# Another order of rows for the first part of x: which 24 KB row of DRAM goes to which partition

## The chip, the cores and the metric

The kernel runs on one core of one Trainium2 chip. The metric is device time in microseconds (us) of one execution; for the kernel before, three runs gave a median of 123.88 us (123.86 to 124.13). The profile is that of one further execution.

## The reference

```
x: (16, 512, 768) f32, A: (768, 16) f32, B: (16, 768) f32, scale = 0.5
out = x + scale * ((x @ A) @ B)        # f32
```

Flattened, x and out have 8192 rows of 768 numbers, 3 KB each. The kernel reads 25.2 MB and writes 25.2 MB.

## The kernel before

The 8192 rows are 64 tiles of 128 rows (one row per partition), and the tiles are taken in five parts of 8, 8, 16, 16 and 16 tiles (PARTS). A part of S tiles is laid out so that partition p holds S consecutive rows of DRAM: in the first two parts 8 rows, which are one run of 24 KB, in the others 16 rows, 48 KB. All of this is in one helper, memory(t2, i, s, n) (L92 to L94), which turns "part i, tiles s to s+n" into a pattern over DRAM; loads of x and stores of out both use it, so a row is stored where it was read.

x_sb has room for 48 tiles. The last part therefore goes into the room of the first two parts once these have been stored.

All transfers are issued by SP, in the order written by hand in on_sync, and one queue takes them in that order:

- the first part of x in two loads: tiles 0 and 1 (6 KB of each partition's 24 KB), then tiles 2 to 7 (18 KB of it); line L135
- A in three small loads of four 4 KB rows (L150) and B in one load of sixteen 3 KB rows (L154); both go to partitions 8 apart
- the second part of x in one load of 24 KB per partition, the third in two such loads, the fourth in one of 48 KB per partition (L135)
- the store of the first part and that of the second, each after the sum of its tiles is done (L143)
- the two loads of the fifth part, each after one of these stores has landed (L135)
- the stores of the third, fourth and fifth parts, 48 KB per partition (L143)

Every load has a semaphore of its own. The other engines work on groups of 8 tiles. For each group, POOL and ACT cast x to f16 (L179), half a group each; DVE transposes the copy in blocks of 32 (L237); TensorE projects it with A into y_ps (L268); ACT scales y and spreads it over a block diagonal y_bd (L225); TensorE multiplies by B into PSUM (L289); DVE adds the result to x in place (L242). A group's work needs no particular row in a particular partition: it treats the 128 rows of a tile alike.

Of the kernel before, what the change touches and what calls it, by code (L numbers as in the profile page):

```python
# [14 lines left out]


GROUP = 8

SUB = 4

# [4 lines left out]
def kernel(  # L25
# [10 lines left out]
    P = 128  # L36
# [7 lines left out]
    NC = D // 64  # L44
    NG = sum(PARTS) // GROUP
    PAIRS = GROUP // 2
    assert sum(PARTS) * P == T and NG * GROUP == sum(PARTS)
    sc = float(scale)


    def sb(name, shape, dtype):
        return nc.alloc_sbuf_tensor(name, shape, dtype).ap()

    def ps(name, shape):
        return nc.alloc_psum_tensor(name, shape, fp32).ap()
# [14 lines left out]
    b_mm = sb("b_mm", [P, D], MM_DT)  # L70
    xn = sb("xn", [P, GROUP, D], MM_DT)
    xt = sb("xt", [P, GROUP, D], MM_DT)
    y_bd = sb("y_bd", [P, GROUP, P], MM_DT)
    lora = [ps(f"lora_ps{i}", [P, 2, D]) for i in range(2)]
# [9 lines left out]
    parts = []  # L84
# [6 lines left out]

    def memory(t2, i, s, n):  # L92
        S = PARTS[i]
        return t2[ds(parts[i], S * P), :].rearrange("(p s) d -> p s d", s=S)[:, ds(s, n), :]  # L94

    def held(i, s, n):
        return tiles(where.index((i, s)), n)
# [34 lines left out]
    def on_sync(e):  # L132
        def load(k):
            ld = LOADS[k]
            e.dma_start(out=held(*ld), in_=memory(x2, *ld)).then_inc(s_load[k], 16)  # L135

        def store(k, done):
            st = STORES[k]
            e.wait_ge(s_sum, k + 1)
            if STORED[k] + 1 < NG:  # L140

                e.sem_inc(s_free[PAIRS - 1], 1)  # L142
            e.dma_start(out=memory(out2, *st), in_=held(*st)).then_inc(done, 16)  # L143
# [226 lines left out]
```

## Time and profile before

| what | value |
|---|---|
| median of three runs | 123.88 us |
| the profiled execution's own time | 123.84 us |
| its span, first to last instruction | 122.0 us |
| TensorE busy | 52.3 us (43%) |
| VectorE (DVE) busy | 81.7 us (67%) |
| ScalarE (ACT) busy | 37.5 us (31%) |
| GpSimd (POOL) busy | 28.8 us (24%) |
| moved by DMA | 50.43 MB in 1928 packets |

The span is 1.8 us shorter than the time, since the time also holds what lies ahead of the first and behind the last instruction. Each transfer of x or out consists of 128 packets, one per partition, of 6, 18, 24 or 48 KB; a core has 16 DMA engines, so an engine moves eight packets of each transfer. The trace records for each packet when it started, how long it took and its size, but not which engine or partition it belongs to. In the groups and in the chain, "SPq" is SP issuing a transfer, and "DMA" is the time from issue to landing, the wait in the queue included.

### The profile page before, as it was taken

The numbers are of one execution on the slowest core, as the hardware profiler recorded it, in microseconds if no ns is written. First come the engines' busy times: TensorE is split into PE (matmuls) and PEld (weight loads), VectorE is DVE, ScalarE is ACT, GpSimd is POOL, SyncE is SP. The second block draws the span as 40 slices with busy tenths as digits, with TensorE's granted clock in tenths as the row PEclk, the third lists the DMA queues.
The fourth block names the chain that finished last, engine by engine and source line by source line (L and its number), as shares of the span: only waits on it lengthen the run. The fifth ranks groups of instructions, "written<-read, shape, count | busy, mean of one in ns | idle before, by whom it ended". The sixth has DMA issues, their size and how long they took to land.

```text
span 122.0 us, 887 instructions
## 1 busy us (share of the span) xinstructions
PE 52.3 (43%) x322; PEld 30.4 (25%) x322; DVE 81.7 (67%) x42; ACT 37.5 (31%) x43; POOL 28.8 (24%) x26
## 2 busy tenths in 40 slices
PE   0000229487457647746745735974674340000000
PEld 0000016253233424424423322642442110000000
DVE  0002950599999999999999989999995991000000
ACT  4002938526409312734440093553004000000000
POOL 7731657127009002604400080530000000000000
PEclk9999999999999999999999996899999955555555
DMA  3999999999997996999999999998998998899890
GB/s 56 431 435 399 443 443 403 443 443 403 516 483 322 483 516 266 459 419 411 459 427 427 443 419 459 451 516 354 419 516 371 403 516 387 387 516 403 371 516 0
DMA packets 1928, 50.43 MB, mean 413 GB/s; under 512 B 236, under 2 KB 236, under 8 KB 392
## 3 DMA queue, kind: packets, MB, share of 16 engines
q1 hardware_dynamic: 1928, 50.43, 96.9%
HBM read 25.26 MB, written 25.17 MB: 413 GB/s over the span
## 4 chain that ended last, share of the span: by engine, by line
DMA 39%; DVE 28%; PE 7%; ACT 3%; issue 3%; POOL 2%; SPq 0%; DVEq 0%
DMA x_sb<-in_x_dram 20%; DMA out_dram<-x_sb 18%; DVE x_sb L242 18%; DVE xt L237 10%; PE ps_yt L268 5%; ACT xn L179 3%; POOL xn L179 2%; PE lora_ps L289 1%; SPq L135 0%; SPq L365 0%; DVEq L255 0%; SPq L130 0%; SPq L142 0%
## 5 line engine op out<-in xcount | busy, mean ns | idle before, releaser
L242 DVE TENSOR_TENSOR x_sb<-x_sb,lora_ps 128x1536 f32<-128x1536 f32 x32 | 53.7, 1735 | 1.4 <-PE lora_ps L289 1.4
L289 PE MATMUL lora_ps<-b_mm,y_bd 128*128 128x512 f16 (+1 forms) x128 | 26.6, 343 | 22.5 <-issue 14.8
L179 ACT CAST xn<-x_sb 128x3072 f16<-128x3072 f32 (+1 forms) x9 | 23.4, 2609 | 36.3 <-DMA x_sb<-in_x_dram 23.7
L268 PE MATMUL ps_yt<-xt,w_bd 128*128 128x256 f16 x192 | 26.5, 291 | 11.4 <-DVE xt L237 11.4
L237 DVE STREAM_TRANSPOSE xt<-xn 128x3072 f32<-128x3072 f32 (+1 forms) x9 | 27.1, 3006 | 6.3 <-PE ps_yt L268 5.5
L179 POOL CAST xn<-x_sb 128x3072 f16<-128x3072 f32 (+1 forms) x8 | 20.7, 2588 | 44.9 <-PE ps_yt L268 22.9
L268 PEld LDWEIGHTS ps_yt<-xt,w_bd 128*128 128x128 f16 x192 | 19.1, 102 | 19.4 <-issue 14.5
L289 PEld LDWEIGHTS lora_ps<-b_mm,y_bd 128*128 128x128 f16 x128 | 11.1, 100 | 35.8 <-issue 17.9
L225 ACT ACTIVATE y_bd<-ps_yt 32x256 f16<-32x256 f32 x32 | 12.0, 375 | 18.6 <-PE ps_yt L268 18.3
L230 DVE STREAM_TRANSPOSE a_t<-a_rows 96x1024 f32<-96x1024 f32 x1 | 1.9, 1946 | 11.5 <-DMA a_rows<-in_A_dram 11.5
L301 PE MATMUL lora_ps<-b_half,pick 128*128 128x512 f16 (+1 forms) x2 | 0.8, 500 | 12.8 <-POOL b_half L197 12.8
L301 PEld LDWEIGHTS lora_ps<-b_half,pick 128*128 128x128 f16 x2 | 0.1, 105 | 12.8 <-issue 12.8
L207 POOL COPY w_bd<-w_one 32x384 f16<-32x384 f16 x4 | 2.0, 502 | 0.2
L197 POOL CAST b_half<-b_rows 128x768 f16<-128x768 f32 x1 | 0.8, 829 | 4.7 <-DMA b_rows<-in_B_dram 4.7
L179 ACT ACT_TABLE_LOAD x1 | 1.3, 1283 | 0.9 <-SPq L130 0.9
L201 POOL CAST w_one<-a_t 32x128 f16<-32x128 f32 x3 | 1.2, 396 | 1.0 <-DVE a_t L230 0.9
L187 POOL MEMSET w_bd<- 128x1536 f32 x1 | 1.4, 1380 | 0.0
L184 POOL MEMSET a_rows<- 96x1024 f32 x1 | 0.9, 948 | 0.5 <-SPq L130 0.5
L218 ACT CAST b_mm<-lora_ps 128x768 f16<-128x768 f32 x1 | 0.8, 800 | 0.0
L185 POOL MEMSET b_rows<- 128x768 f32 x1 | 0.7, 735 | 0.0
L188 POOL MEMSET y_bd<- 128x512 f32 x1 | 0.5, 522 | 0.0
L190 POOL TENSOR_SCALAR_AFFINE_SELECT pick<-pick 128x128 f16<-128x128 f16 x1 | 0.3, 307 | 0.0
(5 smaller groups left out, 0.6 us busy)
## 6 DMA issues: line engine op xcount, KB each, us to landing
out_dram<-x_sb SPq DMA_DIRECT2D x3, 6144.0 KB, 23.6
x_sb<-in_x_dram SPq DMA_DIRECT2D x5, 3072.0 KB, 14.6
x_sb<-in_x_dram SPq DMA_DIRECT2D x1, 6144.0 KB, 41.9
out_dram<-x_sb SPq DMA_DIRECT2D x2, 3072.0 KB, 21.2
x_sb<-in_x_dram SPq DMA_DIRECT2D x1, 2304.0 KB, 10.0
x_sb<-in_x_dram SPq DMA_DIRECT2D x1, 768.0 KB, 4.6
a_rows<-in_A_dram SPq DMA_DIRECT2D x3, 16.0 KB
b_rows<-in_B_dram SPq DMA_DIRECT2D x1, 48.0 KB, 7.7
```

Source lines behind the costliest of these rows:

```text
L179: ins = copy(out=xn[:, ds(first, n), :], in_=tiles(t, n))
L184: e.memset(a_rows[0 : NC * APART], 0.0).then_inc(s_ready, 1)
L187: e.memset(w_bd.rearrange("p c k m -> p (c k m)").bitcast(fp32), 0.0)
L201: e.tensor_copy(out=w_one[:, ds(b * EACH, EACH), :, :], in_=a_t[ds(b * Q, Q)].rearrange("i k r (c n) -> i c k r n", n=APART)[..., 0],).the ...
L207: e.tensor_copy(out=w_bd[ds(b * Q, Q), :, :, ds(b * Q, R)], in_=w_one).then_inc(s_w, 1)
L225: last = e.mul(out=y_bd[q, :, q], in_=y_ps[q, :, :], mul=sc)
L230: e.transpose(out=a_t[0 : NC * APART].rearrange("i k r c -> i (k r) c"), in_=a_rows[0 : NC * APART].rearrange("c (i k r) -> c (k r) i", k= ...
L237: return e.transpose(out=ts[0], in_=ts[1])
L242: ins = e.tensor_tensor(out=xs, in0=xs, in1=lora[p % 2], op=mybir.AluOpType.add)
L268: mm = e.matmul(y_ps, w_bd[:, c, k, :], xv[:, :, c, :, k], start=(m == 0), stop=(m == MMS - 1),)
L289: mms.append(e.matmul(t[:, k, ds(n0, w)], y_bd[:, 2 * p + k, :], b_mm[:, ds(n0, w)], start=True, stop=True,))
L301: last = e.matmul(lora[0][:, 0, ds(n0, w)], pick.rearrange("p b r -> p (b r)"), b_half[:, ds(n0, w)], start=True, stop=True,)
```

## The change

In the helper, the first part (i == 0) gets another pattern. Its 128 runs of 24 KB are counted as j * 16 + e, with e from 0 to 15 and j from 0 to 7, and run j * 16 + e goes to partition e * 8 + j. So runs that are neighbours in memory go to partitions 8 apart, and one partition block of eight takes every sixteenth run. Both loads and the store of the first part change alike; nothing else does. The bytes of each packet, the number of transfers and their order on SP are as before; the pattern on the DRAM side has an outer dimension of 16 (24 KB apart) and a next one of 8 (384 KB apart) where it had one of 128.

```diff
 GROUP = 8
+
+
+ENG = 16
...
     def memory(t2, i, s, n):
         S = PARTS[i]
-        return t2[ds(parts[i], S * P), :].rearrange("(p s) d -> p s d", s=S)[:, ds(s, n), :]
+        rows = t2[ds(parts[i], S * P), :]
+        if i == 0:
+            return rows.rearrange("(j e s) d -> e j s d", s=S, e=ENG)[:, :, ds(s, n), :]
+        return rows.rearrange("(p s) d -> p s d", s=S)[:, ds(s, n), :]
```

## The prediction

> **What bounds the kernel now.** I read the page's DMA rows first, then the stretches of the span, then SP's issues and SP's waits.
>
> ```profile
> DMA  3999999999997996999999999998998998899890
> q1 hardware_dynamic: 1928, 50.43, 96.9%
> ```
>
> One queue keeps the sixteen DMA engines busy in 96.9% of the span. The row of tenths is low only in the first and the last slice. By stretch (the last two columns are the DMA share and GB/s; a share over 1 means that packets overlap):
>
> ```profile
> 0.00:2.00 2.00, 0.00 (x0) 0.00 (x0) 0.00 (x0) 1.09 (x1) 1.25 (x6) 1.00 0.04 6
> 2.00:4.70 2.70, 0.00 (x0) 0.00 (x0) 0.00 (x0) 0.19 (x1) 2.67 (x5) 1.00 1.04 335
> 4.70:10.00 5.30, 0.00 (x0) 0.00 (x0) 0.00 (x0) 0.00 (x0) 1.62 (x2) 1.00 0.98 419
> 10.00:47.00 37.00, 20.25 (x122) 12.02 (x123) 29.58 (x15) 17.68 (x18) 12.27 (x11) 1.00 1.01 429
> 47.00:54.50 7.50, 4.93 (x34) 2.80 (x32) 7.50 (x5) 4.25 (x5) 2.75 (x1) 1.00 1.03 442
> 54.50:120.60 66.10, 27.16 (x169) 15.59 (x168) 44.65 (x24) 14.26 (x19) 8.25 (x3) 0.80 0.99 425
> ```
>
> I cut at transfers: 2.0 to 4.7 is the first load, 4.7 to 10.0 the second, 47.0 to 54.5 the store of the first part, by the packet records. From 10 us on the rate hardly moves, for loads and stores alike. The packet records say why: 18 KB packets take 0.686 us (lowest and median alike), 24 KB packets 0.916, 48 KB packets 1.81, all about 27 GB/s per engine, with hardly any spread. Only the first load is slower: its first sixteen packets, one per engine, take 0.37 to 1.18 us, on average 0.77, where later ones take 0.234.
>
> So the end is set by the transfers from 2.0 us to 120.6 us, and a microsecond added to any of them is added to the end. What could hide it is a wait of the queue for its issuer:
>
> ```profile
> SPq L142 <- DVE x_sb L242: 55.0, 3, 26.1
> SPq L143 <- DVE x_sb L242: 17.6, 1, 17.6
> ```
>
> SP waits for DVE's sums, but is early even so: the chain of waits has the first store issued at 32.9, and its packets start at 47.0, 14.1 us later; the last store is issued at 101.0, and packets of the one before it run to 106.1. So the engines' work has 5 us or more to spare, and it moves along when the loads do. It hides nothing that is added to a transfer, and stays hidden itself.
>
> **The change, part by part.** It touches three transfers of 128 packets, eight per DMA engine: load one, 8 x 0.234 = 1.87 us at the settled rate; load two, 8 x 0.686 = 5.49; the first store, 8 x 0.916 = 7.33. Together 14.7 us of the 118.6 us of transfers. Packets, bytes, instructions of the other engines and SP's order are the same. TensorE, VectorE, ACT and POOL gain and lose nothing.
>
> *Issue.* The pattern of the first part no longer has 128 rows on both sides. The nearest rows are the issues of x (same form on both sides) and those of A and B, with short patterns:
>
> ```profile
> L135 SPq DMA_DIRECT2D x_sb<-in_x_dram x2: 383/398/412, 1.0 to 1.4; - x2
> L150 SPq DMA_DIRECT2D a_rows<-in_A_dram x3: 577/595/757, 1.9 to 3.4; - x3
> L154 SPq DMA_DIRECT2D b_rows<-in_B_dram x1: 542/542/542, 4.0 to 4.0; - x1
> ```
>
> If the new pattern is issued like those of A, an issue costs 595 - 398 = 0.2 us more (bounds: nothing, and 757 - 383 = 0.37). Only the first load's counts: nothing runs ahead of it. Load two's lies beside load one's data; the issues of A, B and the rest (4.0 to 6.6) lie beside load two's, which lasts to 10; the store's has its 14.1 us. Term: **+0.2**.
>
> *Rate of the three transfers.* What changes is who moves what. [...] With 16 outside on the DRAM side, I assume that an engine's share is one e: eight partitions in a row, 8e to 8e+7. The flat durations of before fit sixteen engines that each end in a place of their own. If partitions share entrances into SBUF, blocks of eight in a row may put two engines on one entrance at a time while others stand empty, since all sixteen walk through their blocks in step; each packet then takes twice its row. The trace can't show this directly: it has no engine or partition numbers, and no x transfer with this share.
>
> [...]
>
> Bounds from rows. Upper end: every packet doubles, +14.7. Lower end: nothing, by the row that speaks against: B's sixteen packets go to partitions 8 apart, one from each block of eight, and the records have 14 of them at 0.121 us and two at 0.21, so no doubling as a rule; but they are 3 KB each and spread over 0.9 us, too small and scattered to stand in each other's way for long. Below nothing: the first sixteen packets lose 0.77 - 0.234 = 0.53 us on average, which is all that a friendlier order in DRAM could win, since everything later runs at its settled rate.
>
> I take the upper end, since the loads are the opposite of B: 6 to 24 KB per packet, back to back, all engines in step. From it goes what engines out of step save. The first sixteen packets end between 2.36 and 3.28 us; two engines drawn from such a spread differ by a third of 0.92, 0.3 us. If a pair meets afresh in each half of each of three transfers, that is 6 x 0.3 = 1.8 us; but the end waits for the pair closest in step, so I take half, 0.9. Term: +14.7 - 0.9 = **+13.8**. The later transfers are not slowed: their share is the old one.
>
> Sum, against the profiled execution: 123.84 + 0.2 + 13.8 = **137.8 us**; the median of the runs shown is 0.04 above that execution, which changes nothing.
>
> **Rivals.**
>
> *Collisions on one side only.* Writing into SBUF is slowed, reading from it for the store is not, or the other way round. Loads alone: 123.84 + 0.2 + 7.4 - 0.6 = 130.8; the store alone: 123.84 + 0.2 + 7.3 - 0.3 = 131.0. For it: loads and stores have the same packet times, so the rows can't tell which side sets them. Against it: the same engines and partitions in both.
>
> *The rate stays.* Either the engines keep their old share (the change does not do what it says), or two engines in one block do not hinder each other. Then only the issue is left: 123.84 + 0.2 = 124.0, at most 124.6 if the first packets also start 0.4 us later. For it: B's packets. Against it: nothing in the trace is like the new share under full load.
>
> *Faster.* At the start sixteen engines read addresses 24 KB apart, one stretch of 384 KB, instead of places far apart. If that is what makes the first packets late, up to 0.53 us comes back: 123.84 + 0.2 - 0.53 = 123.5. It decides from the point where it wins more than the issue's 0.2 plus 0.25, so only if nearly all of the loss goes. For it: the slow first sixteen packets. Against it: they look like a first answer from memory, and any order has one.
>
> **How the numbers follow.** Two runs differ by 0.25 us (0.2%) without a cause, so within that counts as the same. Chances: collisions both ways 0.50 (134 to 141: the upper end is the full doubling, plus the 0.37 us issue, plus 2 us for engines that meet others still in the next transfer); one side only 0.16 (126 to 134); the rate stays 0.21, of which 0.11 within 0.25 us and 0.10 slower by more; faster 0.13. So slower 0.50 + 0.16 + 0.10 = 0.76, same 0.11, faster 0.13. The range runs from 123.9, which leaves out "faster" and about half of "same" (0.18), to 141 (0.02 above). The likeliest case's own range is 134 to 141.
>
> **What would show it.** Right: packets of 6, 18 and the store's 24 KB at about twice 0.234, 0.686 and 0.916 us; GB/s near 215 in the stretches of the three transfers, with the DMA share still near 1; the second load landing near 18 us instead of 11.4; later stretches at 425 to 429 GB/s. Issue: the first L141 issue (the load's line then) at 0.6 us instead of 0.4. Wrong: flat packets as before, or a slow start alone; then only the first slices differ, and the time is 123.3 to 124.6.

## The result, and the profile after

The changed kernel takes 137.75 us (median of six runs, 137.23 to 138.79) beside 123.93 for the kernel before on the same chip: 1.112 times as long, interval 1.109 to 1.115. The profiled execution is the longest of the six: 138.79 us, with a span of 137.0. Times and ratios in this document are of fast runs alone; only the kernel with the pattern in all five parts had others, two of six at 217.3 and 219.1 us.

Its page shows the same queue, the same packets and bytes, and DMA engines that are as busy as before. Only the rate has changed, in two places (40 slices of 3.4 us):

```profile
DMA  2998999999999998998999999999999999999970
GB/s 48 273 242 183 198 398 409 445 438 431 409 459 459 459 459 344 344 266 179 337 445 337 373 445 438 366 445 431 431 445 431 416 431 459 445 416 431 431 316 14
q1 hardware_dynamic: 1928, 50.43, 95.8%
```

Counted from 0, slices 1 to 4 hold the two loads of the first part, slices 15 to 18 its store. Busy is not fast here: the DMA row reads 9 in slice 4, at 198 GB/s, as it does in slice 7, at 445. Cut at these transfers, by stretch (the five busy times are those of PE, PEld, DVE, ACT and POOL, each with its count of instructions; then the granted TensorE clock, the DMA share and GB/s):

```profile
2.40:6.20 3.80, 0.00 (x0) 0.00 (x0) 0.00 (x0) 0.00 (x0) 2.42 (x5) 1.00 1.16 273
6.20:17.50 11.30, 0.00 (x0) 0.00 (x0) 0.00 (x0) 0.00 (x0) 1.46 (x1) 1.00 1.00 214
17.50:54.00 36.50, 19.97 (x127) 12.03 (x128) 30.37 (x16) 17.68 (x18) 12.26 (x11) 1.00 0.99 425
54.00:67.00 13.00, 8.18 (x56) 4.91 (x57) 13.00 (x7) 7.00 (x6) 5.50 (x2) 1.00 1.01 278
67.00:92.00 25.00, 10.88 (x58) 6.27 (x56) 16.56 (x9) 5.75 (x9) 2.75 (x1) 0.74 1.01 408
```

The second load (6.2 to 17.5) runs at 214 GB/s where it had 419; the loads behind it are back at 425; the store (54 to 67) runs at 278 where it had 442; and behind the store the rate stays a little low. In the packet records the 18 KB packets went from a median of 0.686 us to 1.43, the 6 KB ones from 0.234 to 0.40, the store's 24 KB ones from 0.912 to 1.47. Eight idle engines beside eight at the old packet times would give half the GB/s too, but the longer packets and the DMA share of 1.00 in the second load exclude that. The first two issues are longer too (383/398/412 ns before):

```profile
L141 SPq DMA_DIRECT2D x_sb<-in_x_dram x2: 573/625/677, 1.0 to 1.7; - x2
```

SP still waits for DVE's sums, and they are still early enough: the last store is issued at 115.6, and the sixteen engines land the one before between 118.2 and 121.6.

Most of the 15.0 us by which the profiled span grew can be added up from the packet records, eight packets per engine and transfer: first packet 0.45 later (1.99 to 2.44); load one 8 x (0.419 - 0.323) = 0.8; load two 8 x (1.387 - 0.692) = 5.6; the store 8 x (1.463 - 0.913) = 4.4; the transfers of 24 KB packets in the second part and the fifth part's loads, together 2.1 (means of 0.97 to 1.00 instead of 0.91 to 0.95); and in the last store the slowest engine lands 2.1 behind the mean of the sixteen instead of 0.7, 1.4 more. Sum 14.7, with unrounded terms; the remaining 0.3 is not accounted for.

### The profile page after: what moved, and what is told of

Same layout as the page of the kernel before. It is cut to its first block, busy times and chain, and to the rows that moved or that the text cites. A ratio compares the mean times of both kernels' runs of the same rounds, so it can differ in the third digit from the quotient of the medians.

```text
span 137.0 us, 887 instructions
## 1 busy us (share of the span) xinstructions
PE 52.3 (38%) x322; PEld 30.8 (22%) x322; DVE 82.0 (60%) x42; ACT 37.5 (27%) x43; POOL 28.8 (21%) x26
## 4 chain that ended last, share of the span: by engine, by line
DMA 48%; DVE 19%; PE 6%; ACT 3%; SPq 3%; issue 3%; POOL 2%; POOLq 0%; DVEq 0%
DMA x_sb<-in_x_dram 27%; DMA out_dram<-x_sb 21%; DVE x_sb L248 14%; DVE xt L243 5%; PE lora_ps L295 4%; PE ps_yt L274 2%; POOL xn L185 2%; ACT xn L185 2%; SPq L156 1%; ACT y_bd L231 1%; SPq L141 1%; SPq L160 0%; SPq L371 0%; POOLq L184 0%; DVEq L261 0%
```

## The experiments

**The theory:** the pattern of 16 by 8 gives each DMA engine eight partitions in a row, and in such a share two engines at a time use one entrance into SBUF, while other entrances stand empty. Both statements are the author's assumptions: the traces show packet times and rates, neither the shares of the engines nor entrances. **The rivals:** the order in DRAM (rows that are neighbours are moved by different engines at once), the form of the pattern (two outer dimensions), something that belongs to the start or to the first part alone, and a longer issue. Each experiment is timed against the kernel before on the same chip (123.9 to 124.0); the ratio is to that time, with its 95% interval.

### Blocks of four partitions

```diff
-ENG = 16
+ENG = 32
```

> The first part's pattern is 32 by 4 in place of 16 by 8: neighbouring rows of DRAM go to partitions 4 apart, and a share can be cut from blocks of four partitions. Still two outer dimensions, still rows taken from all over the first part. If blocks of eight partitions make engines meet at shared entrances of SBUF, they need not meet with blocks of four: packets of 6, 18 and 24 KB back at 0.234, 0.686 and 0.916 us, and 124.1 to 124.5 us, the longer first issue (0.68 in place of 0.38 us) being what is left. If neighbouring rows in different engines, or the pattern's form, cost the time, packets stay at 0.40, 1.43 and 1.47 and the time at 136 to 139 us.

124.52 us, ratio 1.0048 (1.0030 to 1.0067). Its two loads and its store, by stretch:

```profile
2.40:5.20 2.80, 0.00 (x0) 0.00 (x0) 0.00 (x0) 0.00 (x0) 2.41 (x5) 1.00 0.94 285
5.20:10.50 5.30, 0.00 (x0) 0.00 (x0) 0.00 (x0) 0.00 (x0) 1.46 (x1) 1.00 1.05 443
47.60:55.10 7.50, 4.23 (x28) 2.36 (x26) 7.50 (x4) 4.25 (x5) 2.75 (x1) 1.00 1.05 449
```

Full rate in load two and in the store; 18 KB packets are at 0.686 us again. Neighbouring rows still go to partitions that lie apart, the pattern still has two outer dimensions, and the first two issues take 578 and 684 ns, as in the changed kernel (573 and 677). So none of these costs the 13.8 us; what this kernel no longer has is the sixteen blocks of eight. Its order of rows is not quite that of the changed kernel either; a later experiment parts the order from the blocks.

### Two halves, without the new pattern

```diff
+SPLIT = (slice(0, 64), slice(64, 128))
-            e.dma_start(out=held(*ld), in_=memory(x2, *ld)).then_inc(s_load[k], 16)
+            for h in SPLIT if ld[0] == 0 else (slice(None),):
+                e.dma_start(out=held(*ld)[h], in_=memory(x2, *ld)[h]).then_inc(s_load[k], 16)
```

(The same for the store; who waits for these transfers waits for 32.)

> The kernel before, with its own order of rows in DRAM; only each of the three transfers of the first part is issued as two, one for partitions 0 to 63 and one for 64 to 127. If partitions share entrances so that 64 neighbours reach only half of them, all sixteen engines crowd on eight entrances though nothing of the new order is there: packets of 18 KB at 1.37 us, twice 0.686, load two landing near 18 us, and 134 to 140 us in all. If the order in DRAM or the pattern's form is what costs, packets are flat and the time is 124 to 125 us, three more issues of 0.4 us lying beside transfers.

138.76 us, ratio 1.119 (1.115 to 1.123):

```profile
2.30:17.00 14.70, 0.00 (x0) 0.00 (x0) 0.00 (x0) 0.00 (x0) 3.98 (x6) 1.00 1.01 217
17.00:54.00 37.00, 19.93 (x123) 12.02 (x124) 29.76 (x15) 17.68 (x18) 12.26 (x11) 1.00 1.01 427
54.00:67.00 13.00, 8.13 (x55) 4.66 (x53) 13.00 (x8) 7.00 (x6) 5.50 (x2) 1.00 1.00 257
```

The signature of the changed kernel, with nothing of its pattern or its order: 217 GB/s in the loads, 18 KB packets at 1.43 us, the store at 257. What is left in common, if the theory's shares hold, is where in SBUF the engines work at one time. Measured are the rates: 64 neighbouring partitions take about half of what 128 take in the loads (217 GB/s where the kernel before has 335 in load one and 419 in load two; 18 KB packets at 1.43 us where it has 0.686), and six tenths in the store (257 where it has 442). Shared entrances are the author's explanation of this; no trace shows them.

### Even and odd partitions

```diff
-SPLIT = (slice(0, 64), slice(64, 128))
+SPLIT = (slice(0, 128, 2), slice(1, 128, 2))
```

> As the kernel with two halves, but the two transfers take the even and the odd partitions, so that each reaches over all 128: the same count of transfers, packets and issues. If shared entrances are the cause, nothing meets: packets of 18 KB at 0.686 us, 124 to 125 us. If splitting a transfer in two is itself what costs, the time is that of the two halves.

125.93 us, ratio 1.0169 (1.0143 to 1.0196). Most of the halves' price is gone, yet the time lies 1 us above what was expected. The store's packets are flat (0.912, at most 0.964). The loss is in load two: some of its first packets take 1.0 to 2.5 us, and the stretch of 5 to 13 us has 365 GB/s:

```profile
2.30:5.00 2.70, 0.00 (x0) 0.00 (x0) 0.00 (x0) 0.00 (x0) 2.52 (x5) 1.00 0.96 294
5.00:13.00 8.00, 0.00 (x0) 0.00 (x0) 0.00 (x0) 0.00 (x0) 1.46 (x1) 1.00 1.01 365
13.00:47.00 34.00, 18.88 (x112) 11.12 (x113) 26.80 (x14) 17.68 (x18) 12.27 (x11) 1.00 1.02 439
```

Since four issues at the start differ here from before, the pair was run again with the loads as they were, and only the store split.

### Halves, and even and odd, in the store alone

> The kernel before with its own order and pattern; only the store of the first part is issued as two, partitions 0 to 63 and 64 to 127. If 64 neighbouring partitions share half of the entrances, its 24 KB packets take 0.912 to 2.6 us as in the kernel with both halves, and the time is 129.5 to 132 us, as with the new pattern in the store alone (130.8). If it takes the new pattern to slow a store: 123.9.

131.43 us, ratio 1.0585 (1.0567 to 1.0603). The stretch of its store:

```profile
47.00:60.00 13.00, 8.14 (x55) 4.89 (x56) 13.00 (x7) 7.00 (x6) 5.50 (x2) 1.00 1.00 263
```

> The same with the even and the odd partitions: two issues and twice the transfers as well, but each over all 128 partitions. Entrances shared by neighbours: packets at 0.912 and 123.8 to 124.2 us, so that what even and odd loads lost (2.0 us) lies in the loads at the start. If splitting a transfer costs by itself: 125 to 126.

123.97 us, ratio 1.0000 (0.9991 to 1.0010):

```profile
47.00:54.50 7.50, 4.40 (x28) 2.43 (x28) 7.50 (x4) 4.25 (x5) 2.75 (x1) 1.00 0.98 423
```

Two transfers, two issues and 64 partitions each in both kernels; the one has 263 GB/s, the other 423. Splitting costs nothing here; which 64 partitions costs 7.5 us. The two also differ in DRAM: a half is one stretch of 1.5 MB, the even rows are spread over 3 MB. No run parts this for the halves, but the changed kernel, too, spreads its rows over 3 MB and is slow. What the even and odd loads lose at the start is another matter, and stays open.

### A stretch of its own in DRAM for each block

```diff
-        if i == 0:
-            return rows.rearrange("(j e s) d -> e j s d", s=S, e=ENG)[:, :, ds(s, n), :]
+        if i < 2:
+            both = t2[ds(0, 2 * S * P), :].rearrange("(e h j s) d -> h e j s d", s=S, e=ENG, h=2)
+            return both[i][:, :, ds(s, n), :]
```

> Pattern of 16 by 8 again, but now the eight rows of one block of eight partitions are neighbours in DRAM (one stretch of 192 KB), and a block's stretches of the first and the second part alternate; the first two parts have this pattern, since the stretches of one part alone would fold into the old pattern. If blocks of eight partitions are the cause, the order in DRAM does not help, and the second part pays too: load of 24 KB packets at 1.4 to 1.8 us in both parts' stores and the second part's load, 145 to 153 us in all. If neighbouring rows in different engines are the cause, it is gone: 124 to 125 us.

150.50 us, ratio 1.214 (1.212 to 1.216). Load one's tail and load two, the second part's load, the loads behind, and both stores:

```profile
6.20:17.50 11.30, 0.00 (x0) 0.00 (x0) 0.00 (x0) 0.00 (x0) 1.46 (x1) 1.00 1.02 214
17.50:32.00 14.50, 5.41 (x26) 3.20 (x26) 5.28 (x3) 4.92 (x3) 4.01 (x8) 1.00 0.99 207
32.00:61.00 29.00, 15.47 (x93) 9.13 (x94) 24.00 (x12) 12.64 (x15) 8.24 (x3) 0.82 1.02 431
61.00:86.40 25.40, 10.68 (x73) 6.22 (x71) 20.78 (x11) 8.50 (x10) 5.49 (x2) 0.87 0.98 264
```

With eight neighbouring rows of DRAM in each block the loads are as slow as with rows 384 KB apart (214 in both). The order in DRAM is out as a cause. The second part pays as the first does; its load's packets, with a mean of 1.87 us, even lie a little above the 1.4 to 1.8 that was expected.

### Loads alone, store alone

```diff
-    def memory(t2, i, s, n):
+    def memory(t2, i, s, n, new=False):
...
-        if i == 0:
+        if i == 0 and new:
...
-            e.dma_start(out=held(*ld), in_=memory(x2, *ld)).then_inc(s_load[k], 16)
+            e.dma_start(out=held(*ld), in_=memory(x2, *ld, new=True)).then_inc(s_load[k], 16)
```

(For the store alone, new=True stands in the store.)

> The new pattern in the two loads of the first part alone; its store has the old one, so that rows of the first part's output come out in another order. Shared entrances while writing into SBUF: load two lands near 18.4 us as in the changed kernel, the store's packets are at 0.912, and the time is 123.9 + 0.5 (first packet later) + 6.3 (mean extra of the two loads' packets) = 130.5 to 131.5. If only reading for the store were slowed: 124.5.

131.14 us, ratio 1.0579 (1.0562 to 1.0597). Loads of the first part, loads behind them, store:

```profile
2.40:17.50 15.10, 0.00 (x0) 0.00 (x0) 0.00 (x0) 0.00 (x0) 3.87 (x6) 1.00 1.02 226
17.50:54.00 36.50, 20.25 (x123) 12.10 (x124) 29.68 (x15) 17.67 (x18) 12.25 (x11) 1.00 1.00 427
54.00:61.50 7.50, 4.94 (x34) 2.73 (x31) 7.50 (x5) 4.25 (x5) 2.75 (x1) 1.00 1.01 433
```

> The new pattern in the store of the first part alone; again its output rows come out in another order. Shared entrances while reading from SBUF: packets of the store at 0.912 to 2.4 with a mean near 1.46, engines out of step by some 3 us behind it, later transfers slowed a little where engines meet, and 129.5 to 132 us. If only writing is slowed: 123.9, since the store's longer issue lies 14 us ahead of its packets.

130.82 us, ratio 1.0537 (1.0517 to 1.0557). Load two and the store:

```profile
4.70:10.00 5.30, 0.00 (x0) 0.00 (x0) 0.00 (x0) 0.00 (x0) 1.62 (x2) 1.00 1.02 435
47.00:60.00 13.00, 8.12 (x55) 4.72 (x54) 13.00 (x8) 7.00 (x6) 5.50 (x2) 1.00 1.01 278
```

Both directions pay, 7.2 and 6.8 us, and the two add up to the whole (14.0 beside 13.8). They do not pay in the same way. After the two loads the engines land within 0.7 us of each other (17.64 to 18.33; before the change, 10.27 to 11.38); after the store they land between 58.3 and 61.3, and this disorder stays to the end.

### The store in blocks of four

(ENG = 32, and new=True in the store alone.)

> The pattern of 32 by 4 in the store alone (output rows of the first part in another order). Its issue is longer, as in the kernel with blocks of four, but 14 us ahead of its packets. If what is left of blocks of four (0.6 us over before) is the first load's issue, this gives 123.8 to 124.1; if the form of the pattern itself slows transfers, 124.2 or more.

123.93 us, ratio 0.9996 (0.9986 to 1.0005). The pattern of two outer dimensions costs this store nothing (123.93 us beside 123.98); in the kernel before, the store's issue lies 14.1 us ahead of its packets. The 0.6 us that blocks of four cost in the loads as well (124.52) is thus in the loads: their first packet starts 0.44 us later (2.43 instead of 1.99), as the trace of that kernel has it.

### All five parts

```diff
-        if i == 0:
+        if True:
```

> The pattern of 16 by 8 in all five parts. Shared entrances: every load and store pays; loads at twice 58.6 us, stores between 1.6 times and twice 58.6, where loads and stores overlap a little less: 195 to 240 us, with 200 to 270 GB/s throughout. If something of the start or of the first part alone is the cause, 137 to 140.

212.0 us, ratio 1.707 (1.703 to 1.710):

```profile
2.40:100.00 97.60, 32.21 (x160) 18.82 (x161) 40.70 (x21) 22.27 (x24) 19.29 (x19) 0.76 1.01 232
100.00:211.00 111.00, 29.66 (x164) 17.52 (x162) 41.99 (x22) 13.79 (x19) 7.82 (x3) 0.65 0.91 251
```

The price is not bound to the start or to the first part. The 24 KB loads of the second and third part have packets with means of 1.82 to 1.84 us where 0.916 was the row. One transfer pays much less than expected: the store of the first part has packets with a mean of 1.07 us here, where they had 1.46 in the changed kernel. Why is open.

## Why the prediction was right

*What bounds the kernel, and that nothing hides an added microsecond:* right. The sum over the packet records gives 14.7 of the 15.0 us of the profiled execution, and SP's issues stayed ahead of the transfers.

*Issue, +0.2:* too small. The first issue went from 0.38 to 0.68 us, and the first packet starts 0.45 us later; the upper bound of 0.37 was for this issue alone. The prediction put load two's issue beside load one's data, but it ends ahead of the first packet, before the change (1.82 and 1.99) as after it (2.28 and 2.44). It also grew, from 0.41 to 0.57, and the two growths, 0.29 and 0.16, add up to the 0.45. In every kernel here the first packet starts 0.14 to 0.18 us after the end of the second issue; whether it waits for that issue is not shown. The store in blocks of four shows that this is a cost of the loads only.

*Two engines on one entrance, each packet at twice its row:* the longer packets are right in kind, and four kernels part them from the rivals (blocks of four, two halves, a stretch of its own, even and odd in the store). The doubling, which the +14.7 of the sum rests on, was the author's estimate; no run ahead of the forecast showed it. The runs showed in its place means of 0.419 us beside 0.323 in load one, 1.387 beside 0.692 in load two and 1.463 beside 0.913 in the store. That two engines share an entrance is not shown by any trace. That an engine's share in the 16 by 8 pattern is eight partitions in a row remains an inference: no trace has engine numbers. It rests on the equal rates (214 GB/s there, 217 with the two halves). How many engines meet at one entrance at a time, two as assumed or more, is not seen either. The doubled rows were 1.37 for load two; the trace has 1.43, 4% more.

*The saving by engines out of step, 0.3 us per meeting, half of it taken:* right in size for the loads together. The packet records of load two come in waves of sixteen: 1.245, three at 1.42 to 1.43, then 1.28, three more at 1.42 to 1.43 (medians of each wave). Once in four packets 0.15 to 0.19 us is saved against the other three. Loads: 6.8 us forecast (7.4 less four savings of 0.15), 6.3 in the packets of the profile. Term by term it is less good: load one cost 0.8 where 1.6 was forecast, since its packets did not double, the first sixteen least of all (0.77 us on average before, 0.71 after); load two cost 5.6 where 5.2 was forecast.

*The store, +7.0:* too large. Its packets cost 4.4 us. Its engines fall out of step, and a third of its packets run at about 0.912, undisturbed; that the one saves the other is argued, not shown.

*"The later transfers are not slowed: their share is the old one":* wrong. This step failed. The engines leave the store up to 3 us apart, and the three transfers of 24 KB packets behind it cost 1.9 us more in the profile (the other 0.2 of the 2.1 lies ahead of the store, in the second part's load), while the slowest engine lands 1.4 us further behind the mean. That engines out of step meet others at the entrances there is the likeliest reading, not shown. The range had 2 us for this at its upper end, the sum nothing. The store alone, at 6.8 us in all, shows that the two errors nearly cancel: 4.5 in its own packets, the rest behind them. So the total of 137.8 beside 137.75 is in part luck: the three transfers were slowed as forecast in kind, but the agreement to a tenth of a microsecond is not earned.

*B's packets as the row that speaks against it:* rightly set aside. Sixteen packets of 3 KB, spread over 0.9 us, did not show what back-to-back packets show.

## What to carry to other kernels

When a transfer is bound by the DMA engines, look at which partitions it takes and in which order, not only at bytes and packets: a DRAM side whose outer dimension is 16, or a transfer of 64 neighbouring partitions, loaded at half the full rate here (214 and 217 GB/s beside 419 before) and stored at about six tenths of it (278 and 257 beside 442), while 128 (419 and 442) and 32 by 4 (443 and 449) ran at full rate, and so did every second partition in a store (423). The busy share says nothing about it (1.00 at 214 GB/s, 0.98 at 419); GB/s by stretch and the time of one packet do. To try another order of rows in DRAM, keep an outer dimension of 32 or 128, the two that ran at full rate here, and issue the first load of the kernel in the plain form, since its longer issue (0.6 us in all) is not covered.

## What the runs showed of the hardware that was not expected

- The slowed loads and the slowed stores go differently. The loads stay even: with the loads alone the engines land load two 0.7 us apart, where they were 1.1 apart before the change, and the 24 and 48 KB loads of the second to fourth part in the kernel with all five parts keep them within 1.05. The stores do not: some packets run at 0.912 us while others take 1.9 to 2.4, and in the kernel with the store alone the engines land 3.1 us apart. Why is open.
- Behind that disorder later transfers are slower too, though they have the old pattern: 24 KB packets of up to 2.2 us in the next ones, where 0.912 is their median, and at the end a slowest engine 2.1 us behind the mean. With the pattern in all five parts the engines land the last store 14.8 us apart.
- Loads of even and odd partitions at the start lost 2.0 us which the store of the same form did not. Their engines land load two 2.7 us apart, and are still 2.2 apart in the last store; what sets them apart was not followed.
